# An encoder layer on one core: the queries' squared lengths from products with ones instead of from turned queries

## The chip, the core and the metric

The kernel runs on one core of one Trainium2 chip. The time is the device time of one execution in microseconds; the lower the better. A profile of one execution lists each instruction of the engines: TensorE (PE for its matmuls, PEld for its loads of the stationary operand), VectorE (DVE), ScalarE (ACT), GpSimd (POOL), and SyncE (SP), which here only issues transfers. Each engine works through its own queue in order. SBUF holds 128 partitions; PSUM, where TensorE writes, has 8 banks of 2 KB per partition, that is 512 fp32 numbers.

## What is computed

One layer of an encoder over 1040 tokens (16 learned ones ahead of 1024) with 1024 features: an RMS norm, one wide input projection, two mixers side by side (a gated delta rule over 8 heads of 128 features, run forwards and backwards, and a short convolution), a gated merge, an output projection, and a SwiGLU block. All in fp32. The part that matters here is how the delta rule treats its queries and keys:

```python
def l2norm(t):
    return t * lax.rsqrt(jnp.sum(t * t, axis=-1, keepdims=True) + L2_EPS)

    qkv = jax.nn.silu(depthwise_conv_centred(jnp.concatenate([q, k, v], axis=-1), conv_w)).astype(f32)
    qc, kc, vc = jnp.split(qkv, [DN_QK, 2 * DN_QK], axis=-1)
    qc = l2norm(qc.reshape(Bsz, L, DN_HEADS, DN_DK)) * (DN_DK ** -0.5)
    kc = l2norm(kc.reshape(Bsz, L, DN_HEADS, DN_DK))
...
    o = (o_fwd + o_bwd)[:, META_PAD:]
    o = o * lax.rsqrt(jnp.mean(o * o, axis=-1, keepdims=True) + RMS_EPS) * norm_w.astype(f32)
```

So for each head and token the sum of squares over the 128 features is wanted, of the key and of the query. The query's scale passes linearly to the output `o` of its token, so the kernel leaves queries unscaled and brings their squared length in only when `o` is normed, at the end of the head's scan.

## The kernel before

The first part of the kernel, to about 1062 us, holds the input projection and the whole delta rule. The projection is cut into units of 128 output features (`u_qkv`, `u_short`, `u_gate`, `u_z`). `dense_steps` (L332) runs a unit's matmuls, three fp32r products for each of 8 blocks of 1024 features and each stretch of 320 to 512 tokens; its matmuls are L339. The features come out on the partitions and the tokens along the free dimension, so a head's keys and queries lie as `kT` and `qT`, the two halves of the tile `kq`: 128 features by 1040 tokens.

The work of the heads is put between these matmuls. A head passes through four streams, written as generators: `g_decay` (the decay factors `PQ`, 128x2x128 for each of 8 chunks of 128 tokens; exponentials at L532 on ScalarE), `g_norm` (lengths, and the products of keys with keys and of queries with keys), `g_inv` (the inverse of a triangular block for each chunk, on VectorE with transfers through DRAM, then 32x32 and 64x64 products at L711 to L749) and `g_scan` (the recurrence; matmuls L805 to L840). At each `yield` a stream names the time at which it wants to go on. After each three projection matmuls `run_streams` (L967) resumes every stream whose time has come, and `pump` (L316) hands VectorE jobs of its own (convolutions, the small triangular solves). All of that happens while the program is being written: the times come from the planner's own estimates, kept in `T` by `pe`, `V`, `A` and `on`, and what results is a fixed order of instructions on each engine. The hardware then keeps each engine's order, and semaphores make it wait for what is not ready.

`g_norm` (L537) goes like this. The 16 learned tokens are turned first (L561, L562). Then `tok` (L553) is called for each of four pairs of chunks: it takes a PSUM bank by `psd` (three banks in turn) and turns two chunks of keys and two of queries into it, by TensorE transposes (`transpose`, L97), so that tokens lie on the partitions. ScalarE copies the two turned chunks of keys to `kn` (L580), which the scan needs, and squares all four with a running sum along the free dimension (L550, 128x128, followed by the reading of the accumulator), into the columns `ssk` and `ssq` of `small`. The turned queries are used for nothing else. One `tok` runs ahead of ScalarE's work on the one before.

`kkq` (L587) multiplies a chunk's keys with the chunk's keys and queries together: one fp32 product, 128 stationary columns, 256 moving ones, into a bank by `psd`. Two run ahead (L593). The loop over chunks (L606 to L621) then waits for the chunk's exponentials, has VectorE form the two `NP` blocks from the bank (L612) and multiply `PQ` by its second half (L616), and issues the `kkq` of two chunks on. `ssk` goes into `cc` ahead of the loop (L595 to L599). `ssq` is first read in `norm` at the end of `g_scan` (L883).

Two pools matter beside: `half_buffer` (L351), three buffers of 128x520 in SBUF, taken in turn by the tanh of the convolutions (L366), the short convolutions' sums (L409, L414), the gates (L458) and others; and SyncE's queue, in which the weight loads (L935) stand among the transfers of `g_inv` and the stores.

Of the kernel before, what the change touches and what calls it, by code (L numbers as in the profile page):

```python
# [8 lines left out]
F32 = mybir.dt.float32  # L9
F32R = mybir.dt.float32r  # L10
I32 = mybir.dt.int32
AF = mybir.ActivationFunctionType
# [4 lines left out]
P = 128  # L17
# [3 lines left out]
META = 16  # L21
# [4 lines left out]
NC = 8  # L26
# [21 lines left out]
def encoder_layer(ctx: ExitStack, tc: tile.TileContext, x, meta, norm1_w, w_in, w_ba,  # L48
                  dn_conv_w, A_log, dt_bias, dn_norm_w, sc_conv_w, w_bdn, w_bsc,
                  w_out, norm2_w, w_gu, w_down, final_w, out):  # L50
    nc = tc.nc
# [8 lines left out]
    dr = ctx.enter_context(tc.tile_pool(name="dr", bufs=1, space=DRAM))  # L60
# [3 lines left out]
    def uid(s):  # L64
        cnt["n"] += 1
        return f"{s}_{cnt['n']}"

    def s4(n=1024):
        return tp.tile([P, 1024], F32, tag="s4", name=uid("s4"), bufs=4)[:, :n]
# [4 lines left out]
    def psd():  # L74
        return ps.tile([P, 512], F32, tag="e", name=uid("pe"), bufs=3)
# [18 lines left out]
    mm = nc.tensor.matmul  # L94

    def transpose(dst, src, n=P):
        nc.tensor.transpose(dst, src, ident[:n, :n])  # L97
# [167 lines left out]
    def on(e, ns, ready=0.0):  # L265

        T[e] = max(T[e], ready, T["pe"]) + ns
        return T[e] + TOPE

    def pe(ns):  # L270
        T["pe"] += ns
        return T["pe"] + HOP

    def V(n, kind=0):
        return on("dve", (68 + 1.042 * n, 130 + 1.042 * n, 130 + 0.52 * n)[kind])

    def A(n):
        return on("act", 144 + 0.834 * n)
# [19 lines left out]
    def enqueue(lane, gen):  # L298
        j = Job(gen)
        if not lanes[lane]:  # L300
            spent[lane] = max(spent[lane], min(spent.values()))
        lanes[lane].append(j)
        return j
# [47 lines left out]
    def half_buffer():  # L351
        return d1.tile([P, 520], F32, tag="rb", name=uid("rb"), bufs=3)
# [129 lines left out]
    def cs(c):  # L482
        return slice(META + c * P, META + (c + 1) * P)

    B = lambda b: slice(32 * b, 32 * b + 32)
# [16 lines left out]
    def norm_job(st_, ssk1, cc, ce, he, y, tmp, sk):  # L502
        nc.vector.tensor_tensor(out=ce, in0=cc, in1=he, op=ALU.mult)
        V(18)
        yield T["dve"] + DEP
        rsqrt(y, ssk1, tmp)
        [V(9) for _ in range(11)]
        yield T["dve"] + DEP
        nc.vector.tensor_tensor(out=sk, in0=y, in1=ssk1, op=ALU.mult)
        V(9)  # L510
# [25 lines left out]
    def g_norm(h, st_):  # L536

        kq = st_["kq"]
        kT, qT = kq[:, 0], kq[:, 1]
        small = dn.tile([P, 9, 12], F32, tag="small", name=uid("small"), bufs=2)  # L540
        st_["small"] = small
        ssk, ssq, rk2, ssk1, y, tmp, sk = (small[:, :, i] for i in range(7))
        cc, ce = small[:, :, 7:9], small[:, :, 9:11]
        nc.gpsimd.memset(small, 1.0)
        kn = dn.tile([P, 9, P], F32, tag="kn", name=uid("kn"), bufs=2)
        st_["kn"] = kn

        def square(src, dst, p=P):
            jk = dn.tile([P, P], F32, tag="jk", name=uid("jk"))
            nc.scalar.activation(jk[:p], src, AF.Square, accum_out=dst)  # L550
            return on("act", 400)

        def tok(c2):  # L553
            pt = psd().rearrange("p (c a d) -> p c a d", c=2, a=2)
            for c in range(2):
                for a, s in ((0, kT), (1, qT)):
                    transpose(pt[:, c, a], s[:, cs(2 * c2 + c)])
            return pt, pe(4 * 107)

        pt = psd()  # L560
        transpose(pt[:META, :P], kT[:, 0:META])  # L561
        mm(pt[:META, P:P + META], kT[:, 0:META], kT[:, 0:META], start=True, stop=True)  # L562
        t = pe(120)
        nxt = tok(0)
        yield t
        nc.scalar.copy(kn[:META, 8], pt[:META, :P])
        A(P)
        square(pt[:META, :P], ssk[:META, 8:9], META)
        Nm = dn.tile([META, META], F32, tag="Nm", name=uid("Nm"), bufs=2)
        st_["Nm"] = Nm  # L570
        nc.scalar.copy(Nm, pt[:META, P:P + META])
        A(META)
        nc.gpsimd.tensor_tensor(out=Nm, in0=Nm, in1=Dm[:, h], op=ALU.mult)
        yield T["act"]
        for c2 in range(4):
            pt, t = nxt
            if c2 < 3:
                nxt = tok(c2 + 1)
            yield t
            nc.scalar.copy(kn[:, 2 * c2:2 * c2 + 2], pt[:, :, 0])  # L580
            A(256)
            for c in range(2):
                for a, s in ((0, ssk), (1, ssq)):
                    t = square(pt[:, c, a], s[:, 2 * c2 + c:2 * c2 + c + 1])
            yield T["act"]

        def kkq(c):  # L587
            pk = psd()
            mm(pk[:, :2 * P].rearrange("p (a t) -> p a t", a=2), kT[:, cs(c)], kq[:, :, cs(c)],  # L589
                                  start=True, stop=True)  # L590
            return pk, pe(435)

        nxt = [kkq(0), kkq(1)]  # L593
        yield T["act"] + HOP
        nc.vector.tensor_scalar(out=ssk1, in0=ssk, scalar1=EPS, scalar2=None, op0=ALU.add)  # L595
        nc.vector.reciprocal(rk2, ssk1)
        hb = beta.rearrange("p c (d h) -> p c d h", d=2)[:, :, :, h]
        he = ed.rearrange("p c (d h) -> p c d h", d=2)[:, :, :, h]
        nc.vector.tensor_tensor(out=cc, in0=hb, in1=rk2.unsqueeze(2).broadcast_to([P, 9, 2]), op=ALU.mult)  # L599
        nc.vector.tensor_scalar(out=Nm, in0=Nm, scalar1=cc[:META, 8, 0:1], scalar2=None, op0=ALU.mult)  # L600
        on("dve", 500)
        NP = dn.tile([P, NC, 2, P], F32, tag="NP", name=uid("NP"), bufs=2)
        PQ = st_["PQ"]
        st_["NP"] = NP
        yield T["act"] + HOP - 300
        for c in range(NC):  # L606
            pk, t = nxt.pop(0)
            while c not in st_["exp"]:
                yield T["pe"] + 200
            yield max(t, st_["exp"][c])  # L610
            for d in range(2):
                nc.vector.scalar_tensor_tensor(out=NP[:, c, d], in0=pk[:, 0:P], scalar=cc[:, c, d:d + 1],  # L612
                                               in1=PQ[:, c, d], op0=ALU.mult, op1=ALU.mult)
                V(P, 1)
            yield T["dve"] - 200
            nc.vector.tensor_tensor(out=PQ[:, c], in0=pk[:, P:2 * P].unsqueeze(1).broadcast_to([P, 2, P]), in1=PQ[:, c],  # L616
                                    op=ALU.mult)
            V(2 * P)
            if c + 2 < NC:
                nxt.append(kkq(c + 2))  # L620
            yield T["dve"] - 200  # L621
        enqueue("norm", norm_job(st_, ssk1, cc, ce, he, y, tmp, sk))
# [325 lines left out]
    def start_streams():  # L948
        nonlocal ndec, nnorm, ninv, nscan
        h = ndec  # L950
        if h < H and h < freed + 2 and not decs:
            decs.append([g_decay(h, heads[h]), T["dve"] + HOP, h])
            ndec += 1
        h = nnorm
        if h < H and h < ndec and h < done + 2 and not norms and all(k in heads[h] and heads[h][k]() for k in ("tk", "tq")):
            norms.append([g_norm(h, heads[h]), T["dve"] + HOP, h])
            nnorm += 1
        h = ninv
        if h < H and not invs and heads[h].get("normed"):
            invs.append([g_inv(h, heads[h]), T["dve"] + HOP, h])  # L960
            ninv += 1
        h = nscan
        if h < H and not scans and heads[h].get("inverted") and "tv" in heads[h] and heads[h]["tv"]():
            scans.append([g_scan(h, heads[h]), T["dve"] + HOP, h])
            nscan += 1
# [22 lines left out]
    with tc.tile_pool(name="st", bufs=1) as st:  # L988
# [9 lines left out]
        rows = st.tile([P, 2, P], F32, name="rows")  # L998
# [208 lines left out]
        ones = c1.tile([P, P], F32, name="ones")  # L1207
# [336 lines left out]
    t = KT - 1  # L1544
# [99 lines left out]
    rows = [s4(D) for _ in range(4)] + [rows2[:, t] for t in range(4)]  # L1644
# [129 lines left out]
```

## Time and profile before

| | us |
|---|---|
| Three runs, median | 2010.35 (2009.24 to 2010.55) |
| The profiled execution | 2009.61 |
| its span, first instruction to last | 2007.9 |
| TensorE busy | 1987.4 |
| VectorE busy | 1353.8 |
| ScalarE busy | 823.9 |
| GpSimd busy | 119.6 |

How to read the rows that follow. In the first row the busy time of each engine stands with its share of the span and the number of instructions. A row of a stretch gives the window's start and end, its length, and for PE, PEld, DVE, ACT and POOL the busy time and the number of instructions, then the granted TensorE clock (1.00 is full speed), the share of the DMA engines' time and GB/s. A row of a group names line, engine, operation, out and in, shapes and count, then after a bar the busy time together and the mean of one in ns, then the engine's idle time before them and what ended it. A row of a wait has who waited for whom, the total in us, how often, and the longest. A row of the timeline gives start, duration, engine, line and operation; rows of one kind that follow each other are merged (x4). A matmul's record is longer than the time by which it holds TensorE, as the next one starts while it drains; what it costs is read from the end of one to the end of the next. An fp32 product leaves two matmul records, an fp32 transpose one.

### The profile page before, as it was taken

What the parts mean: (1) busy time and instruction counts of PE and PEld (TensorE: products, weight loads), DVE (VectorE), ACT (ScalarE), POOL (GpSimd) and SP (SyncE); (2) the same over time, 40 slices, a digit from 0 to 9 for tenths busy, and PEclk for the clock granted to TensorE, in tenths of its full rate; (3) what the DMA queues carried; (4) which work ended last, traced back from release to release, by engine and by line L of the source; (5) the groups of instructions that cost most, each with busy time, mean ns of one, the idle gap of its engine ahead of it and who ended that gap; (6) DMA issues with size and microseconds to landing.
All of it is one profiled execution on the core that took longest, in us unless ns stands there. A gap on an engine that the chain in (4) does not pass through costs nothing.

```text
span 2007.9 us, 31943 instructions
## 1 busy us (share of the span) xinstructions
PE 1987.4 (99%) x12059; PEld 1727.9 (86%) x12059; DVE 1353.8 (67%) x2966; ACT 823.9 (41%) x1945; POOL 119.6 (6%) x407
## 2 busy tenths in 40 slices
PE   9999999999999999999999999999999999999998
PEld 8999999999999988988888888887888888888887
DVE  6889586888888776866245434468866666646575
ACT  6462345454554464633334211224423333334344
POOL 2002200101020202010000000000000000000000
PEclk9999999999999999999999999999999999999999
DMA  3121222212212232232127633123666345477654
GB/s 138 40 88 64 75 78 71 74 47 76 59 54 85 69 101 64 81 89 94 70 94 247 215 126 116 58 90 109 237 225 221 139 149 186 158 272 244 196 172 167
DMA packets 131409, 247.85 MB, mean 123 GB/s; under 512 B 45045, under 2 KB 54694, under 8 KB 128823
## 3 DMA queue, kind: packets, MB, share of 16 engines
q1 hardware_dynamic: 130679, 244.77, 36.1%
q8 instruction: 94, 1.54, 0.3%
q10 hardware_dynamic: 576, 1.05, 0.1%
q14 instruction: 60, 0.49, 0.1%
HBM read 179.10 MB, written 66.67 MB: 122 GB/s over the span
## 4 chain that ended last, share of the span: by engine, by line
PE 90%; DVE 5%; ACT 2%; DMA 1%; issue 1%; SPq 0%; ACTq 0%; DVEq 0%
PE pm L339 36%; PE pd L1514 10%; PE pe L1514 4%; PE pm L1514 3%; PE pe L589 1%; PE pd L820 1%; PE pe L134 1%; PE pe L135 1%; PE pe L133 1%; PE pd L840 1%; PE pd L134 1%; PE pd L133 1%; PE pd L135 1%; PE pe L1682 1%; PE pe L1680 1%; PE pd L837 1%
## 5 line engine op out<-in xcount | busy, mean ns | idle before, releaser
L339 PE MATMUL pm<-hTh,wh 128*128 128x512 f32 (+4 forms) x1424 | 518.2, 369 | 0.8 <-ACT kq L391 0.5
L339 PE MATMUL pm<-hTh,wl 128*128 128x512 f32 (+4 forms) x1424 | 483.4, 344 | 0.0
L339 PE MATMUL pm<-al,wh 128*128 128x512 f32 (+4 forms) x1424 | 482.6, 343 | 0.0
L339 PEld LDWEIGHTS pm<-hTh,wh 128*128 128x128 f32 x1424 | 267.0, 188 | 20.4 <-issue 1.7
L339 PEld LDWEIGHTS pm<-hTh,wl 128*128 128x128 f32 x1424 | 266.1, 188 | 19.8 <-DVE wl L942 0.3
L339 PEld LDWEIGHTS pm<-al,wh 128*128 128x128 f32 x1424 | 267.4, 189 | 14.5
L101 DVE TENSOR_TENSOR al<-raw,ring_h 128x1024 fp32r<-128x1024 f32 x73 | 88.8, 1224 | 65.4 <-ACT ring_h L100 64.6
L942 DVE TENSOR_TENSOR wl<-raw,wh 128x512 fp32r<-128x512 f32 x134 | 91.0, 690 | 51.0 <-ACT wh L945 50.5
L100 ACT CAST ring_h<-raw 128x1024 fp32r<-128x1024 f32 x73 | 76.8, 1055 | 106.8 <-PE pd L1682 35.5
L361 DVE SCALAR_TENSOR_TENSOR kq<-ra,wc,kq 128x520 f32<-128x520 f32 x128 | 96.9, 757 | 3.3 <-ACT kq L391 1.7
L945 ACT CAST wh<-raw 128x512 fp32r<-128x512 f32 x134 | 79.2, 622 | 13.3 <-PE pm L339 9.6
L100 ACT CAST wh<-raw 128x1024 fp32r<-128x1024 f32 x43 | 45.2, 1052 | 85.8 <-PE pe L134 35.2
L827 ACT ACTIVATE w<-pd,small 128x128 f32<-128x128 f32 x128 | 40.2, 366 | 84.8 <-PE pd L820 79.7
L498 DVE TENSOR_TENSOR fP<-fP,tm 128x135 f32<-128x135 f32 (+23 forms) x248 | 71.3, 288 | 4.9
L494 DVE TENSOR_TENSOR tm<-fP,fN 128x135 f32<-128x135 f32 (+23 forms) x248 | 71.2, 287 | 4.4
L849 DVE SCALAR_TENSOR_TENSOR S<-S,eGl,pd 128x128 f32<-128x128 f32 x104 | 31.9, 345 | 52.0 <-PE pd L837 33.9
L1516 DVE TENSOR_TENSOR b<-pd,b 128x512 f32<-128x512 f32 x22 | 15.2, 691 | 68.5 <-PE pd L1514 68.5
L1617 ACT ACTIVATE b<-b 128x512 f32<-128x512 f32 x22 | 13.9, 633 | 114.8 <-DVE b L1516 114.8
L101 DVE TENSOR_TENSOR wl<-raw,wh 128x1024 fp32r<-128x1024 f32 x43 | 52.4, 1220 | 12.3 <-ACT wh L100 12.2
L664 POOL TENSOR_TENSOR tm<-mP,mN 1x15 f32<-1x15 f32 (+7 forms) x120 | 42.9, 358 | 218.7 <-DMA mN<-ndm 210.2
L1514 PE MATMUL pd<-b_hl,wh 128*128 128x512 f32 x176 | 54.4, 390 | 0.0
L361 DVE SCALAR_TENSOR_TENSOR vT<-ra,wc,vT 128x520 f32<-128x520 f32 x64 | 48.4, 756 | 3.6 <-ACT vT L391 2.6
(523 smaller groups left out, 4416.9 us busy)
## 6 DMA issues: line engine op xcount, KB each, us to landing
raw<-in_w_in_dram SPq DMA_DIRECT2D x72, 512.0 KB
raw<-in_w_gate_up_dram SPq DMA_DIRECT2D x44, 512.0 KB
sums<-in_w_down_dram SPq DMA_DIRECT2D x22, 512.0 KB
t_d<-sums SPq DMA_DIRECT2D x11, 1024.0 KB
raw<-s_d SPq DMA_DIRECT2D x44, 256.0 KB
raw<-t_d SPq DMA_DIRECT2D x44, 256.0 KB
act_d<-b SPq DMA_DIRECT2D x43, 256.0 KB
raw<-act_d SPq DMA_DIRECT2D x33, 256.0 KB
```

The costliest lines, as they stand in the source:

```text
L100: nc.scalar.copy(hi, src)
L101: nc.vector.tensor_tensor(out=lo, in0=src, in1=hi.bitcast(F32), op=ALU.subtract)
L133: mm(po[:m, :n], wh[:, k, :m], xhk[:, t0:t0 + n], start=(k == 0), stop=False)
L339: mm(po[:, :n], ww[:, k], f(k)[:, t0:t0 + n], start=i == 0, stop=i == 3 * KT - 1)
L361: nc.vector.scalar_tensor_tensor(out=acc, in0=raw[:, h0 + t:h0 + t + hn], scalar=wc[:, t, col:col + 1], in1=acc, op0=ALU.mult, op1=ALU.add)
L494: nc.vector.tensor_tensor(out=tv, in0=fP[:, 0:r, j:j + 1].broadcast_to([P, r, n]), in1=fN[:, j:j + 1, j + 1:32].broadcast_to([P, r, n]), o ...
L498: nc.vector.tensor_tensor(out=fP[:, 0:r, j + 1:32], in0=fP[:, 0:r, j + 1:32], in1=tv, op=ALU.subtract)
L664: nc.gpsimd.tensor_tensor(out=tv, in0=mP[:, 0:j + 1, j:j + 1].broadcast_to([1, j + 1, n]), in1=mN[:, j:j + 1, j + 1:META].broadcast_to([1, ...
L827: nc.scalar.activation(w[d], b1[:, 2 + d], AF.Copy, scale=ce[:, c, d:d + 1])
L942: nc.vector.tensor_tensor(out=u[1][1][:, k], in0=u[2][:, k], in1=u[1][0][:, k].bitcast(F32), op=ALU.subtract)
L945: nc.scalar.copy(u[1][0][:, k], u[2][:, k])
L1514: mm(po, x[:, k], y, start=k + i == 0 and not add_to, stop=k == 3 and i == 2, skip_group_check=add_to)
```

## The change

`tok` turns keys only, four chunks to a bank, in two calls instead of four; ScalarE copies 512 columns at a time to `kn` and squares four chunks of keys. The queries' squared lengths come from a new generator, `norms_of_q`, started ahead of the loop over chunks and resumed once at the head of each step from the second on, for three resumptions:

- step 1: two squares on ScalarE of 512 tokens each of the unturned `qT`, into two buffers of `half_buffer`;
- step 2: a bank by `psd`, and 8 fp32 products. The stationary operand is 128x32 ones, the moving one 128 tokens of squares; product j of each 512 tokens writes to partitions 32j to 32j+31, so that every row of a group of 32 holds the sums over the features for 128 tokens;
- step 3: a copy of the 256 columns to a third buffer, a transfer of one row per group to a DRAM tile `sq_d`, and a transfer back from `sq_d` into the column `ssq` of `small`, 128 partitions of 8 single numbers.

What the generator yields is not looked at: it is resumed where the loop stands.

```diff
-        def tok(c2):
-            pt = psd().rearrange("p (c a d) -> p c a d", c=2, a=2)
-            for c in range(2):
-                for a, s in ((0, kT), (1, qT)):
-                    transpose(pt[:, c, a], s[:, cs(2 * c2 + c)])
+        def tok(c4):
+            pt = psd().rearrange("p (c d) -> p c d", c=4)
+            for c in range(4):
+                transpose(pt[:, c], kT[:, cs(4 * c4 + c)])
             return pt, pe(4 * 107)
+
+        def norms_of_q():
+            sqs = []
+            for i in range(2):
+                sqs.append(half_buffer()[:, :512])
+                nc.scalar.activation(sqs[i], qT[:, META + 512 * i:META + 512 * i + 512], AF.Square)
+                A(512)
+            yield
+            pq = psd()[:, :256].rearrange("p (i t) -> p i t", i=2)
+            for i in range(2):
+                for j in range(4):
+                    mm(pq[B(j), i], ones[:, 0:32], sqs[i][:, j * P:(j + 1) * P], start=True, stop=True)
+            pe(500)
+            yield
+            rows = half_buffer()[:, :256]
+            nc.scalar.copy(rows.rearrange("p (i t) -> p i t", i=2), pq)
+            A(256)
+            sq_d = dr.tile([2, 4, P], F32, name=uid("sq_d"), tag="sq_d", bufs=2)
+            nc.sync.dma_start(sq_d.rearrange("i j t -> j i t"), rows[0:P:32].rearrange("j (i t) -> j i t", i=2))
+            nc.sync.dma_start(ssq[:, 0:NC], sq_d.rearrange("i j t -> t (i j)"))
+            yield
...
-        for c2 in range(4):
+        for c4 in range(2):
             pt, t = nxt
-            if c2 < 3:
-                nxt = tok(c2 + 1)
+            if c4 < 1:
+                nxt = tok(c4 + 1)
             yield t
-            nc.scalar.copy(kn[:, 2 * c2:2 * c2 + 2], pt[:, :, 0])
-            A(256)
-            for c in range(2):
-                for a, s in ((0, ssk), (1, ssq)):
-                    t = square(pt[:, c, a], s[:, 2 * c2 + c:2 * c2 + c + 1])
+            nc.scalar.copy(kn[:, 4 * c4:4 * c4 + 4], pt)
+            A(512)
+            for c in range(4):
+                square(pt[:, c], ssk[:, 4 * c4 + c:4 * c4 + c + 1])
             yield T["act"]
...
+        late = norms_of_q()
         for c in range(NC):
+            if c:
+                next(late, None)
             pk, t = nxt.pop(0)
```

## The prediction

> **What bounds the kernel now.** I read the page's first part, then the busy time by stretch, then what TensorE itself waited for.
>
> ```profile
> PE 1987.4 (99%) x12059; PEld 1727.9 (86%) x12059; DVE 1353.8 (67%) x2966; ACT 823.9 (41%) x1945; POOL 119.6 (6%) x407
> 105.00:873.00 768.00, 764.04 (x6061) 704.56 (x6062) 609.28 (x1718) 373.02 (x1198) 96.86 (x331) 1.00 0.23 71
> 873.00:1062.00 189.00, 189.00 (x1232) 158.42 (x1229) 87.72 (x274) 71.15 (x197) 9.76 (x32) 1.00 0.27 89
> PE pd L820 <- DVE r L815: 3.4, 6, 0.8
> PE pm L339 <- ACT kq L391: 0.5, 2, 0.3
> PE pd L837 <- ACT v L832: 0.2, 1, 0.2
> ```
>
> The stretch 105 to 873 us holds all eight passes through `g_norm`, the only code that changes. TensorE is busy 764.0 of its 768 us at a granted clock of 1.00, ScalarE only 373. So a nanosecond put on TensorE's queue here, or a wait in it, is a nanosecond of the kernel, while time taken off ScalarE pays nothing unless TensorE was waiting for it. The list of TensorE's waits says that it almost never was: 0.5 and 0.2 us. From 873 to 1062 us TensorE runs without a gap on fill units, so no head's tail is exposed at the end of the phase.
>
> **The change part by part.** *Transposes removed.* Per head 8 of the 16 transposes of L97 go (the queries'), 64 in all. One group of four, between projection matmuls (start, duration):
>
> ```profile
> 108.77 0.31 PE L339 MATMUL pm<-hTh,wl 128*128 128x320 f32 x1
> 108.92 0.60 PE L97 MATMUL pe<-ident,kq 128*128 128x128 f32 x4
> 109.27 0.39 PE L339 MATMUL pm<-hTh,wh 128*128 128x320 f32 x1
> 109.50 0.31 PE L339 MATMUL pm<-al,wh 128*128 128x320 f32 x1
> ```
>
> From the end of the one projection matmul (109.08) to the end of the next (109.66) is 0.58 us, of which that next one alone takes 0.15 (109.50 to the start of its successor). Four transposes cost 0.43, one 0.109; 64 cost 7.0 us.
>
> *Products added.* Per head 8 fp32 products: stationary 128x32 ones, 128 moving columns, each to one of four 32-partition column groups, two rounds of four. What an fp32 product costs at full width is in the keys-by-keys product of L589, 256 moving columns, two records:
>
> ```profile
> 128.59 0.34 PE L339 MATMUL pm<-hTh,wl 128*128 128x384 f32 x1
> 128.77 0.59 PE L589 MATMUL pe<-kq 128*128 128x256 f32 x2
> 129.01 0.53 PE L339 MATMUL pm<-hTh,wh 128*128 128x384 f32 x1
> ```
>
> End to end 0.61, less 0.17 for the last: 0.44 for 256 columns, 0.22 for 128. Twice a transpose: eight in a row would be 1.75 us, against 0.87 for the eight transposes removed. So the part pays only if the groups run at once. The nearest rows are the 32x32 products of the block inverse, which use four column groups too, but also four row groups:
>
> ```profile
> 214.74 0.34 PE L339 MATMUL pm<-hTh,wl 128*128 128x384 f32 x1
> 215.01 0.21 PE L711 MATMUL pd<-XT,NP 32*32 32x32 f32 x1
> ...
> 215.57 0.19 PE L711 MATMUL pd<-XT,NP 32*32 32x32 f32 x1
> 215.69 0.45 PE L339 MATMUL pm<-hTh,wh 128*128 128x384 f32 x1
> ...
> L711 PE MATMUL pd<-XT,NP 32*32 32x32 f32 x32 | 0.8, 194 | 0.0
> L711 PE MATMUL pd<-Xe,NP 32*32 32x32 f32 x32 | 0.7, 194 | 0.0
> ```
>
> 64 records start within 0.56 us, 0.009 each, where a quarter of 0.109 would be 0.027 one after another: at least three ran at once. The whole excursion takes 1.06 us (215.08 to 216.14) less 0.17, that is 0.89; the 0.33 beyond the 0.56 is the price of going into the small tiles and out. I take both over: two rounds of 0.22 plus 0.33 are 0.77 a head, 6.2 us, net −0.8. Bounds: without the mode price 3.5 us (net −3.5); with groups that share the rows and so run one after another, 1.75 + 0.33 a head, 16.6 us (net +9.6). I take the first value, since the columns are what keeps outputs apart in L711 as well.
>
> The Trainium skill ("TensorE: Matmul & The Clock Gate", Part 3, measured speedup vs the span model) gives 2.38x for three column tiles of 32, not three or four. By that the eight products would be 1.75/2.38 = 0.74 instead of 0.44, and the sum 2.4 us higher, an estimate; no run so far shows column groups alone.
>
> *ScalarE.* The costs of what goes and comes:
>
> ```profile
> L550 ACT ACTIVATE jk<-pe 128x128 f32<-128x128 f32 x128 | 35.8, 279 | 3.0
> L550 ACT ACTIVATION_READ_ACCUMULATOR jk<-pe 128x1 f32 x128 | 25.3, 197 | 0.0
> L580 ACT COPY kn<-pe 128x256 f32<-128x256 f32 x32 | 11.6, 363 | 0.1
> L904 ACT COPY NP<-pd 128x512 f32<-128x512 f32 x16 | 9.0, 583 | 15.2 <-PE pd L97 15.1
> L1737 ACT ACTIVATE b<-mA 128x512 f32<-128x512 f32 x4 | 2.5, 627 | 0.0
> ```
>
> Gone: 64 squares with their accumulator reads (64 x 0.476 = 30.5) and 32 copies of 0.363 (11.6). Added: 16 copies of 512 (9.3), 16 squares of 512 (10.0), 8 copies of 256 (2.9). ScalarE loses 20 us of 373, none of it on the path. Zero.
>
> *A new wait at the products.* TensorE's queue is in order, and the products stand in it at the start of step 2 of the loop over chunks. They need two 0.63 squares that ScalarE was given at the start of step 1, and a PSUM bank whose last reader is step 1's multiplication of `PQ` on VectorE (L616). Until now the matmul that waits there waits for the reader of a step further back. How late is that reader? The last head, where steps are shortest:
>
> ```profile
> 857.78 0.59 PE L589 MATMUL pe<-kq 128*128 128x256 f32 x2
> 858.91 0.59 PE L589 MATMUL pe<-kq 128*128 128x256 f32 x2
> 860.03 0.59 PE L589 MATMUL pe<-kq 128*128 128x256 f32 x2
> ...
> 857.96 0.42 DVE L616 TENSOR_TENSOR PQ<-pe,PQ 128x256 f32<-128x256 f32 x1
> 858.93 0.42 DVE L616 TENSOR_TENSOR PQ<-pe,PQ 128x256 f32<-128x256 f32 x1
> 859.91 0.42 DVE L616 TENSOR_TENSOR PQ<-pe,PQ 128x256 f32<-128x256 f32 x1
> ...
> 281.40 0.60 DVE L815 SCALAR_TENSOR_TENSOR r<-pd,negEG,vS 128x128 f32<-128x128 f32 x2
> 282.06 0.71 PE L820 MATMUL pd<-r,NP 128*128 128x128 f32 x4 [0.75 <-DVE r L815]
> ```
>
> It ends 0.60, 0.44 and 0.30 us after its step's key product starts (858.38 against 857.78, and so on); the last two rows give 0.06 for the hop. In the changed program's order the new products stand 0.43 to 1.33 us of TensorE work behind that key product, in three of eight heads the minimum 0.43. That is 0 to 0.2 us late. The squares add more where a step is only 1.1 us long and four exponentials precede them (heads 1, 5, 7). I take 0.2 a head, 1.6 us; bounds 0 and 8.
>
> *A new wait one step later.* The next user of the products' bank is the key product of step 2 or 3; it waits for ScalarE's copy of the sums (0.36). Behind it on TensorE stand the projections. In the changed order it follows the products' end by 0.52, 0.68, 3.5, 1.7, 4.8, 0.52, 2.05 and 0.68 us of TensorE work (heads 0 to 7). With ScalarE free the copy needs 0.06 + 0.36 + 0.06 = 0.48, so it just fits; but ScalarE is in order as well, and between squares and copy stand other things:
>
> ```profile
> L390 ACT COPY ra<-pm 128x320 f32<-128x320 f32 x24 | 10.2, 427 | 6.7 <-PE pm L339 6.7
> 163.01 1.29 ACT L532 ACTIVATE PQ<-PQ,negG 128x128 f32<-128x128 f32 x4 [2.60 <-DVE PQ L527]
> ACT PQ L532 <- DVE PQ L527: 14.5, 15, 2.6
> ACT Xe L691 <- DMA NP<-pd: 19.1, 4, 7.7
> 860.83 0.41 ACT L691 COPY Xe<-NP 32x256 f32<-32x256 f32 x1 [5.16 <-DMA NP<-pd]
> ```
>
> Head 0: two evictions (0.43 and 0.54) and two exponentials (1.29 for four), 1.6 us, against 1.3 from the products' start: 0.7 late with copy and hop. Head 1: four exponentials behind a mask addition (14.5/15, about 1 us): 1.2 late. Heads 5 and 7: two exponentials and the same wait: 0.5 each. Head 3: a copy that waits for a product 1.2 us after the sums: 0.5. Heads 4 and 6: the three block copies of L691 to L693, which today wait for a DMA in four heads of eight, 19.1 us in all; in head 6 then a gate's tanh and four exponentials too: 2.5 late without the DMA; head 4 has 4.8 us of cover: 0. Sum 5.9 us; lower bound 0, upper 5.9 plus 5.16 for each of the two, 16.
>
> *SyncE and DMA.* Per head two small transfers, a write to DRAM and a read back of 1024 single values. The second waits in SyncE's queue for the first to land, and a weight load stands behind it:
>
> ```profile
> SPq L679 <- DMA pd<-fP: 34.8, 11, 6.5
> 172.35 7.80 SPq L935 DMA_DIRECT2D raw<-in_w_in_dram  x2
> 182.54 0.62 ACT L945 CAST wh<-raw 128x512 fp32r<-128x512 f32 x1
> ```
>
> Such a wait takes 34.8/11 = 3.2 us, at most 6.5; the load issued at 172.35 is first read at 182.54, 10 us later. Zero; with the cover gone, a late cast delays the next unit by up to 3 us. The sums' consumer is the end of the head's scan, tens of microseconds on. VectorE and GpSimd get no instruction more or less.
>
> *Order.* The planner issues by its own estimates, which change, so the other streams shift. TensorE's old waits in the scans (3.4 + 0.2) may fall or double: 0, bounds ±3.6.
>
> **Sum.** −0.8 + 1.6 + 5.9 = +6.7 on the profiled execution's 2009.61 (its span 2007.9 and 1.7 around it): 2016.3. The median shown, 2010.35, is 0.74 higher: 2017.
>
> **The rivals.** *Groups one after another* (the products decide, from the point where fewer than two run at once): +9.6 in place of −0.8, 2027. For: all four read the same 128 partitions, which no row shows. Against: L711. *The waits are covered*, ScalarE being 20 us lighter and the order planned: −0.8 and at most 2 us of waits, 2010 to 2012, no change. For: 0.5 and 0.2 us of waits for ScalarE today. Against: the planner's books do not hold the products for the squares, nor the next key product for the copy. *Faster*: the waits are covered, the mode price is half, and the shifted scans lose their 3.4 us for VectorE: −2.1 − 3.4, 2005. For: those waits are accidents of placing. Against: nothing in the change aims at them. *ScalarE held by a DMA* in heads 4 and 6: two times 5.16, 2027, on the forecast's side.
>
> **How the numbers follow.** Forecast with its own range 2014.4 to 2024: 0.55. One after another 0.08, the held ScalarE 0.06, no change 0.19, faster 0.12. Four microseconds, 0.2%, is about what a measurement of this kernel can tell from no change. Slower: 0.55 less 0.03 that falls short, plus 0.14: 0.66. Same: 0.22. Faster: 0.12. The range 2008 to 2027 leaves out most of the faster case and the top of the two expensive ones.
>
> **What would show it.** In the profile after: the time between projection matmuls around the ones products, 0.77 if groups overlap, 2.1 if not; in TensorE's waits new rows at the products (for squares or `PQ`) and at the key product (for the copy), together 7 us, most in heads 0, 1 and 6; ScalarE near 804 us busy. The forecast is wrong if these rows sum to under 3 us, or if a weight cast waits for its load.

## The result, and the profile after

| | before | after |
|---|---|---|
| median of the runs | 2010.35 (2009.24 to 2010.68) | 2029.48 (2028.20 to 2032.07) |
| ratio, 95% interval | | 1.0097 (1.0083 to 1.0112) |
| profiled execution's span | 2007.9 | 2026.6 |

The change costs 19.1 us. First the page's part of busy times, then the busy time by stretch for the stretch that holds `g_norm` (from, to, length, then busy time and count of PE, PEld, DVE, ACT and POOL, the granted clock, the DMA share and GB/s), then TensorE's waits in the order of their sum (total, times, longest). All are of the changed kernel, whose lines behind the edit stand 23 further down: the key product is L609, the products with ones L570, the copy of their sums L574, the multiplication of `PQ` L639, the block copies L714 to L716.

```profile
PE 1993.0 (98%) x12123; PEld 1726.7 (85%) x12123; DVE 1353.0 (67%) x2966; ACT 811.1 (40%) x1825; POOL 118.5 (6%) x407
```

```profile
105.00:873.00 768.00, 750.28 (x5869) 688.25 (x5868) 602.49 (x1704) 356.41 (x1069) 95.29 (x329) 0.99 0.23 70
```

```profile
PE pe L609 <- ACT rb L574: 10.7, 3, 6.1
PE pd L843 <- DVE r L838: 4.0, 10, 0.7
...
PE pe L609 <- DVE PQ L639: 1.8, 2, 1.1
...
PE pm L339 <- ACT kq L391: 0.3, 1, 0.3
PE pe L570 <- DVE PQ L639: 0.3, 1, 0.3
```

In the stretch TensorE now stands idle for 17.7 us, where it was 4.0, and its clock is no longer 1.00 throughout. The first row is the largest part of the loss: three waits of the key product for ScalarE's copy of the sums, 10.7 us, two of them long. The first long one, in head 6, in the timeline (start, duration, engine, line, what; in brackets the idle time before it and what ended it): TensorE, then ScalarE.

```profile
749.46 0.39 PE L339 MATMUL pm<-hTh,wl 128*128 128x512 f32 x1
755.91 1.22 PE L609 MATMUL pe<-kq 128*128 128x256 f32 x2 [6.06 <-ACT rb L574]
756.57 0.99 PE L339 MATMUL pm<-hTh,wh 128*128 128x512 f32 x1
757.36 0.63 PE L339 MATMUL pm<-al,wh 128*128 128x512 f32 x1
...
758.99 0.39 PE L339 MATMUL pm<-hTh,wl 128*128 128x512 f32 x1
759.22 0.39 PE L339 MATMUL pm<-hTh,wh 128*128 128x512 f32 x1
```

```profile
744.97 0.61 ACT L968 CAST wh<-raw 128x512 fp32r<-128x512 f32 x1
751.45 0.41 ACT L714 COPY Xe<-NP 32x256 f32<-32x256 f32 x1 [5.87 <-DMA NP<-pd]
...
752.79 0.60 ACT L458 ACTIVATE rb<-pm 128x512 f32<-128x512 f32 x1
754.33 1.28 ACT L532 ACTIVATE PQ<-PQ,negG 128x128 f32<-128x128 f32 x4 [0.94 <-DVE PQ L527]
755.51 0.35 ACT L574 COPY rb<-pe 128x256 f32<-128x256 f32 x1
```

The copy itself waits for nothing. It is late because ScalarE is in order: block copies of the head before stand in front of it and wait 5.87 us for their transfer, and a gate's tanh and four exponentials come between. The second long wait, in head 7, has the same victim and another cause:

```profile
859.53 0.69 ACT L532 ACTIVATE PQ<-PQ,negG 128x128 f32<-128x128 f32 x2 [1.12 <-DVE PQ L527]
864.51 0.37 ACT L574 COPY rb<-pe 128x256 f32<-128x256 f32 x1 [4.28 <-DMA tb_d<-rb]
```

```profile
864.93 1.22 PE L609 MATMUL pe<-kq 128*128 128x256 f32 x2 [4.35 <-ACT rb L574]
```

Here it is the copy's destination. `rows` is one of the three `rb` buffers that turn, and the one whose turn it is still holds a gate's output that is being stored to `tb_d`.

Both waits cost more than their idle time. The busy time in stretches of 5 us, columns as above, shows the granted clock in the eleventh place:

```profile
750.00:755.00 5.00, 0.00 (x0) 0.00 (x0) 3.79 (x9) 2.48 (x7) 0.00 (x0) 0.71 0.46 103
755.00:760.00 5.00, 4.09 (x12) 3.32 (x13) 3.29 (x10) 0.86 (x4) 0.00 (x0) 0.61 0.42 106
760.00:765.00 5.00, 5.00 (x175) 3.88 (x174) 0.61 (x2) 0.52 (x2) 0.47 (x4) 1.00 0.00 0
...
865.00:870.00 5.00, 5.00 (x16) 4.04 (x17) 2.57 (x8) 1.39 (x4) 0.00 (x0) 0.69 0.45 54
870.00:875.00 5.00, 5.00 (x24) 4.12 (x23) 4.78 (x13) 2.03 (x5) 0.00 (x0) 1.00 0.14 52
```

After each idle stretch the clock is 0.61 and 0.69, and the key product takes 1.22 instead of 0.59. From its start at 755.91 to the projection at 758.99, 3.08 us pass for one key product and five projections; at full speed they take 0.44 + 5 x 0.23 = 1.6. That is 1.5 us more, and in head 7 about as much again. The waits of 1.1 us are followed by no drop. The kernel before has a drop as well, in a later part of the program, behind three waits close together, of 2.63, 0.63 and 0.32 us between 1390.2 and 1395.2:

```profile
1395.00:1400.00 5.00, 4.83 (x16) 3.92 (x17) 3.85 (x7) 1.25 (x2) 0.00 (x0) 0.72 0.70 262
```

So the clock can fall without one long wait. The Trainium skill ("TensorE: Matmul & The Clock Gate", Part 1) says that an idle window of about 3.4 us sets the clock back to half. The drops after 6.06 and 4.35 us and the clock of 1.00 after 1.1 us agree with that; the drop behind three waits, the longest of 2.63 us, says that it is not the least length of one wait.

So the two waits account for 10.4 us idle and some 3 us of slow clock. That leaves near 6 us which no single row of this profile shows.

### The profile page after: what moved, and what is told of

It reads as the page before. It is cut to its first block, busy times and chain, and to the rows that moved or that the text cites. A ratio compares the mean times of both kernels' runs of the same rounds, so it can differ in the third digit from the quotient of the medians.

```text
span 2026.6 us, 31985 instructions
## 1 busy us (share of the span) xinstructions
PE 1993.0 (98%) x12123; PEld 1726.7 (85%) x12123; DVE 1353.0 (67%) x2966; ACT 811.1 (40%) x1825; POOL 118.5 (6%) x407
## 4 chain that ended last, share of the span: by engine, by line
PE 81%; DVE 10%; DMA 3%; ACT 3%; issue 1%; POOL 0%; SPq 0%; ACTq 0%; DVEq 0%; POOLq 0%
PE pm L339 30%; PE pd L1537 10%; PE pe L1537 4%; PE pm L1537 3%; PE pe L134 1%; PE pe L133 1%; PE pe L135 1%; PE pd L843 1%; PE pe L609 1%; PE pd L134 1%; PE pd L133 1%; PE pd L135 1%; PE pe L1705 1%; PE pe L1704 1%; PE pe L1703 1%
## 5 line engine op out<-in xcount | busy, mean ns | idle before, releaser
L339 PE MATMUL pm<-hTh,wh 128*128 128x384 f32 (+4 forms) x1424 | 520.0, 370 | 0.6 <-ACT kq L391 0.3
L339 PE MATMUL pm<-hTh,wl 128*128 128x384 f32 (+4 forms) x1424 | 483.5, 344 | 0.0
L339 PE MATMUL pm<-al,wh 128*128 128x384 f32 (+4 forms) x1424 | 483.1, 344 | 0.0
L101 DVE TENSOR_TENSOR wl<-raw,wh 128x1024 fp32r<-128x1024 f32 x43 | 52.4, 1218 | 13.8 <-ACT wh L100 13.7
L609 PE MATMUL pe<-kq 128*128 128x256 f32 x128 | 39.4, 401 | 12.6 <-ACT rb L574 10.7
```

The lines of the kernel that those rows point to most:

```text
L101: nc.vector.tensor_tensor(out=lo, in0=src, in1=hi.bitcast(F32), op=ALU.subtract)
L339: mm(po[:, :n], ww[:, k], f(k)[:, t0:t0 + n], start=i == 0, stop=i == 3 * KT - 1)
```

## The experiments

Each ratio is against runs of the kernel before on the same chip; the median of these was between 2009.5 and 2010.0. A difference in us between two runs is that of their medians.

**Whose wait is it? (free_bank, own_rows, no_transfers, no_lengths)** Four edits of the changed kernel. *free_bank* cuts the tie between the products' bank and the copy:

```diff
-            nc.scalar.copy(rows.rearrange("p (i t) -> p i t", i=2), pq)
+            nc.scalar.copy(rows.rearrange("p (i t) -> p i t", i=2), sqs[0][:, :256].rearrange("p (i t) -> p i t", i=2))
```

> ScalarE's copy behind the ones products reads the squares in SBUF instead of the sums in PSUM; every instruction, transfer, buffer and the order on each engine stay, the sums of the queries' squares are not read (the queries' lengths are left out of the result). Only the tie between the products' bank and that copy is gone. Theory (TensorE's key product waits for the bank until the copy, and the copy waits in ScalarE's order): the rows of the key product behind L574 vanish; of the 14.7 us that the key products take longer than before and the 1.0 us of slow clock behind them, about 2 us come back in head 6, where the next key product then waits for VectorE, itself held by the transfer NP<-pd: 2013 to 2017 us. Rival (the products and the change of tile size on TensorE cost the time) and rival (the two small transfers cost it) and rival (the replanned order costs it): all of that is still there, 2027 to 2030 us.

Measured: 2015.66, ratio 1.0032 (1.0019 to 1.0045). TensorE's waits, from its list:

```profile
PE pd L843 <- DVE r L838: 3.8, 10, 0.7
...
PE pe L609 <- DVE PQ L639: 2.0, 2, 1.1
...
PE pm L339 <- DVE wl L965: 1.1, 1, 1.1
```

No row of L609 behind L574 is left, and 13.8 us are gone, with every instruction still there. What comes back is as expected in size, but half of it in a place that was not named: a projection waits for the low part of its weight tile, because VectorE too was held by `NP<-pd`.

*own_rows* gives the copy a destination of its own:

```diff
-            rows = half_buffer()[:, :256]
+            rows = dn.tile([P, 256], F32, tag="rq", name=uid("rq"), bufs=1)
```

> The copy of the sums writes a buffer of its own instead of one of the three that turn (rb); nothing else changes, and nothing is left out. Theory: in head 7 the copy waited 4.28 us for a gate's store out of rb, and TensorE 4.35 us behind it; that goes, with about 0.6 us for the key product at half speed and 1.2 us of slow clock after it: 6 us less, 2023 to 2024 us, and in head 6 the wait of 6.06 us stays. Rival (the copy is late in both heads because ScalarE as a whole is held, whatever the buffer): 2028 to 2030 us, and the wait in head 7 stays above 3 us.

Measured: 2024.14, ratio 1.0070 (1.0055 to 1.0085), 5.3 us less and just above its range. TensorE's waits, then two stretches, the first in head 6 and the second in head 7:

```profile
PE pe L609 <- ACT rq L574: 6.1, 2, 5.8
```

```profile
755.00:760.00 5.00, 4.52 (x11) 3.60 (x12) 2.88 (x9) 0.43 (x2) 0.00 (x0) 0.54 0.39 102
...
865.00:870.00 5.00, 5.00 (x24) 4.01 (x23) 2.99 (x8) 2.97 (x7) 0.00 (x0) 1.00 0.47 65
```

Head 6 keeps its wait and its slow clock, head 7 loses both: the slow clock follows the idle time, not the place in the program.

*no_transfers* leaves out the two transfers of the sums:

```diff
-            nc.sync.dma_start(sq_d.rearrange("i j t -> j i t"), rows[0:P:32].rearrange("j (i t) -> j i t", i=2))
-            nc.sync.dma_start(ssq[:, 0:NC], sq_d.rearrange("i j t -> t (i j)"))
```

> The two transfers of the sums (to DRAM and back into ssq) are left out, so the queries' lengths do not reach the result; the copy, the products and the order on TensorE, VectorE and ScalarE stay. Theory: the transfers of head 6 are issued after the wait that costs 6.06 us, so they cannot be its cause: 2027 to 2030 us, both long waits of the key product still there. Rival (the small transfers delay NP<-pd or a weight load): both waits shrink below 2 us and the time falls below 2020 us.

Measured: 2029.57, ratio 1.0099 (1.0084 to 1.0114). The transfers cost nothing.

*no_lengths* leaves out squares, products, copy and transfers, and keeps the buffers, the banks and the planner's books.

> All of the queries' lengths are left out: no squares, products, copy or transfers, while buffers, banks and the planner's books stay, so the remaining instructions come in the changed kernel's order. It prices the removal alone. Theory: the 64 transposes that went are worth 6 to 7 us, the scans' waits in the new order cost up to 2 us: 2003 to 2006 us. Rival (the replanned order costs the time): 2010 us or more.

Measured: 2011.32, ratio 1.0008 (0.9999 to 1.0017). A miss, and it shows where the other 6 us are: without any of the new work, and with 64 transposes fewer, the kernel is no faster than before. What is left of the change is the order of everything else, with the keys' transposes four to a bank: that must cost what the transposes save.

**The order by itself (old_order_keys).** In the kernel before, the queries' transposes and squares are left out while their entries in the planner's books stay, so that all else is issued as before.

```diff
-                for a, s in ((0, kT), (1, qT)):
+                for a, s in ((0, kT),):
                     transpose(pt[:, c, a], s[:, cs(2 * c2 + c)])
...
-                for a, s in ((0, ssk), (1, ssq)):
-                    t = square(pt[:, c, a], s[:, 2 * c2 + c:2 * c2 + c + 1])
+                t = square(pt[:, c, 0], ssk[:, 2 * c2 + c:2 * c2 + c + 1])
+                on("act", 400)
```

> The kernel before with the queries' transposes and their squares left out (the queries' lengths are left out of the result) and nothing else: the planner's books are kept, so that every other instruction stands in the order of before. The same removal in the order of after (no_lengths) gave 2011.32. Theory formed on that run (the removal is worth its transposes, and the new order gives that back through late weight casts in heads 6 and 7, 2.7 us, waits in the scans, 1.7, and at the key products, 2.0): here 7 us less than before, 2002 to 2004 us. Rival (the transposes were covered, their removal is worth nothing in any order): 2008 to 2011 us.

Measured: 2004.83, ratio 0.9974 (0.9965 to 0.9983). The time is just above its range. The removal is worth 5.2 us against the kernel before, most of the 7.0 expected, and the order of after costs 2011.32 − 2004.83 = 6.5 us. This order includes the keys' transposes four to a bank; no run separates the two. The profiled executions allow a look at the first part of the program alone, from the start of the first projection matmul to the end of the last: 16.77 to 1061.11 in the kernel before, 18.21 to 1055.04 in old_order_keys, 17.61 to 1062.48 in no_lengths. That is 7.5 us for the removal and 8.0 for the order; what lies outside differs by about 2 us from one of them to another.

In TensorE's lists of waits, no_lengths has these rows:

```profile
PE pd L843 <- DVE r L838: 3.9, 10, 0.7
...
PE pe L609 <- DVE PQ L639: 2.3, 3, 1.1
...
PE pm L339 <- DVE wl L965: 1.4, 1, 1.4
PE pm L339 <- ACT wh L968: 0.8, 1, 0.8
```

and old_order_keys has only the first of them, at its own line:

```profile
PE pd L820 <- DVE r L815: 3.5, 6, 1.0
...
PE pm L339 <- ACT kq L391: 0.3, 1, 0.3
```

These rows differ by 4.9 us: 2.3 at the key product, 2.2 at projections that wait for weights, 0.4 in the scans. All of TensorE's idle time in the stretch differs by 5.4 us, 9.03 in no_lengths against 3.61 in old_order_keys:

```profile
105.00:873.00 768.00, 758.97 (x6026) 697.35 (x6025) 610.30 (x1731) 350.34 (x1055) 93.44 (x331) 1.00 0.24 71
```

```profile
105.00:873.00 768.00, 764.39 (x6065) 703.68 (x6064) 613.93 (x1734) 351.81 (x1074) 96.49 (x331) 1.00 0.24 72
```

What goes beyond that is not TensorE waiting there, and no run shows where it comes from. In head 6, where the wait for the low weights (wl) and one of those at the key product lie, VectorE is late: in the new order it is given the block work long before its transfer has landed. Its waits for `NP<-pd`, in no_lengths and in the kernel before:

```profile
DVE XT L718 <- DMA NP<-pd: 12.3, 5, 5.6
```

```profile
DVE XT L695 <- DMA NP<-pd: 6.4, 4, 2.8
```

**Do the four column groups run at once? (one_group)** As free_bank, but all eight products write partitions 0 to 31. Their bank is cut into four slots of 128 sums for that.

```diff
-                    mm(pq[B(j), i], ones[:, 0:32], sqs[i][:, j * P:(j + 1) * P], start=True, stop=True)
+                    mm(pq[B(0), j], ones[:, 0:32], sqs[i][:, j * P:(j + 1) * P], start=True, stop=True)
```

> As free_bank (2015.66), but all eight ones products write one column group, partitions 0 to 31, so that they cannot run at once; the sums are not read (the queries' lengths are left out of the result). Theory (four column groups run at once, as the starts of the 16 records in the profile say): the products take 8 x 0.22 + 0.33 = 2.1 us a head in place of 0.77, 1.3 us a head more, 2025 to 2027 us. Rival (the groups took turns anyway, and the products were cheap for another reason): 2014 to 2018 us.

Measured: 2023.84, ratio 1.0071 (1.0057 to 1.0084), 8.2 us above free_bank and below its range, which lay 9 to 11 above. In head 0 the changed kernel, then one_group, between projections:

```profile
124.46 0.34 PE L339 MATMUL pm<-hTh,wl 128*128 128x384 f32 x1
124.73 0.64 PE L570 MATMUL pe<-rb,ones 128*32 128x128 f32 x16
125.31 0.44 PE L339 MATMUL pm<-hTh,wh 128*128 128x384 f32 x1
```

```profile
124.84 0.34 PE L339 MATMUL pm<-hTh,wl 128*128 128x384 f32 x1
125.11 1.93 PE L570 MATMUL pe<-rb,ones 128*32 128x128 f32 x16
126.97 0.44 PE L339 MATMUL pm<-hTh,wh 128*128 128x384 f32 x1
```

From end to end less 0.17 for the projection: 0.78 against 2.06 us, the predicted 0.77 and 2.08. If the four groups run fully at once, the changed kernel takes the time of two products here and one_group that of eight. The difference of 1.28 us is then six products, 0.21 each, close to the 0.22 read from the key product. The 1.3 us a head, 10.2 in all, are there; that the time rose by only 8.2 fits in part the row of the weight wait, which had cost free_bank 1.1 us and is missing here.

**The copy ahead of the block copies (copy_first, copy_first_own).** In the changed kernel ScalarE's copy is issued right behind the products instead of one step later; the order of the other engines stays. copy_first_own has the buffer of own_rows as well.

```diff
             pe(500)
-            yield
             rows = half_buffer()[:, :256]
             nc.scalar.copy(rows.rearrange("p (i t) -> p i t", i=2), pq)
+            yield
             A(256)
```

> The changed kernel with one instruction moved: ScalarE's copy of the sums is issued right behind the products instead of one step later. The order on TensorE, VectorE and SyncE is the same; on ScalarE only the eight copies move ahead, in head 6 ahead of the three block copies that wait for NP<-pd. Nothing is left out. Theory: the wait of 6.06 us in head 6 goes, with 0.6 us of the slow key product and 1.1 us of slow clock, and about 1 to 3 us come back there as late weight casts and as a wait for VectorE, both held by the same transfer (free_bank showed them); in head 7 the copy still waits for the buffer rb, 4 us: 2023 to 2027 us. Rival (head 6 waits for the transfer itself, wherever the copy stands): 2028 to 2031 us with a wait of 5 us or more in head 6.

> copy_first and own_rows together: the copy of the sums right behind the products, into a buffer of its own. Nothing is left out. Theory: both long waits gone without taking the tie away, so the time comes to that of free_bank (2015.66): 2015 to 2019 us, no wait of the key product for ScalarE above 1 us. Rival (the tie itself costs, also with a timely copy): 2020 us or more.

Measured: copy_first 2022.69, ratio 1.0061 (1.0044 to 1.0078), just below its range; copy_first_own 2016.51, ratio 1.0030 (1.0019 to 1.0041). ScalarE of copy_first_own in head 6:

```profile
746.03 0.37 ACT L573 COPY rq<-pe 128x256 f32<-128x256 f32 x1 [2.08 <-PE pe L570]
749.62 0.41 ACT L715 COPY Xe<-NP 32x256 f32<-32x256 f32 x1 [3.22 <-DMA NP<-pd]
```

The block copies still wait for their transfer, but the copy is out by then, and TensorE has no wait for it anywhere. Two small edits take off 13.0 of the 19.1 us without leaving anything out.

**The products behind the last key product (last_steps, old_order_late).** The three parts of `norms_of_q` move into the last three steps of the loop: in last_steps with the planner of after, in old_order_late with the books of before, as in old_order_keys.

```diff
-            if c:
+            if c > 4:
                 next(late, None)
```

> The changed kernel with the three parts of the queries' lengths placed in the last three steps of the loop over chunks: the products come behind the head's last key product, so that no key product of that head waits for their bank. Nothing is left out. Theory: no row of the key product behind L574 over 1 us; what is left is what free_bank showed (late weight casts and VectorE held by NP<-pd), and the order shifts once more: 2008 to 2016 us. Rival (the waits come from ScalarE being behind, wherever the products stand): 2022 to 2030 us, with TensorE's longest wait for ScalarE's copy over 3 us at whatever uses the bank next.

> The changed kernel's way of finding the queries' lengths in the order of before: the planner's books as before, the queries' transposes and squares out, squares, products, copy and transfers put into the last three steps of the loop over chunks, so that no key product of the head stands behind the bank. Nothing is left out. Theory: old_order_keys (2004.83) plus 0.77 us a head, 6.2 us, and up to 3 us of waits for the squares (last_steps showed 1.6 and 0.7): 2011 to 2014 us. That would say that the method is worth nothing against the transposes even in the best place. Rival (the method itself is cheaper and only the new order cost time): 2004 to 2008 us.

Measured: last_steps 2016.75, ratio 1.0030 (1.0018 to 1.0042), a little above its range; old_order_late 2010.17, ratio 1.0000 (0.9991 to 1.0009), between its two. In both no key product waits for the copy. With the products in the same place, the order of after costs 6.6 us more than that of before. In the order of before, the change's way of finding the lengths costs as much as the transposes that it replaces.

**The block copies given out later (late_blocks).** One number of the planner in `g_inv`:

```diff
-        yield T["pe"] + 5600
+        yield T["pe"] + 11600
         yield from take("inv")
```

> The changed kernel with the planner's allowance between the issue of NP<-pd and the block copies raised from 5600 to 11600 of its ns; nothing else is edited, though the planner then places other work anew as well. Nothing is left out. Theory (in head 6 ScalarE and VectorE were given the block copies 6 us before their transfer had landed): their waits for NP<-pd fall below 3 us in all, the long wait of the key product in head 6 goes, and unless the new places hold one of their own the time falls by 6 us or more: 2013 to 2024 us. Rival (the transfer is late because of something that moves with it, so a later place only moves the wait): 2027 to 2032 us, with a wait of 5 us or more for NP<-pd on ScalarE.

Measured: 2012.06, ratio 1.0011 (1.0001 to 1.0021), better than its range. ScalarE's list has no wait for `NP<-pd` left, VectorE's this one and one of 0.2:

```profile
DVE XT L718 <- DMA NP<-pd: 1.0, 1, 1.0
```

That the whole order shifts with this number is part of the result: the scans' waits fell as well, from 4.0 to 1.7 us, so not all of the 17.4 us can be put down to the block copies.

**Another way to the sums (columns_bf16).** In the order of before, the squares are rounded to bf16 and made the stationary operand, 128 squares by 128 tokens; the moving operand is one column of ones. Each product then leaves 128 sums on 128 partitions, where `ssq` wants them.

```diff
...
+            if c == 5:
+                pq = nxt[-1][0][:, 256:264]
+                for i in range(NC):
+                    mm(pq[:, i:i + 1], qs[:, i * P:(i + 1) * P], ones_b[:, 0:1], start=True, stop=True)
+            if c == 6:
+                nc.scalar.copy(ssq[:, 0:NC], pq)
...
```

> A candidate in the order of before: the squares of the queries are written in bf16, each chunk's 128 squares by 128 tokens are the stationary operand of one product with a single column of ones, so that the eight sums of a head land with the tokens on the partitions, in spare columns of the last key product's bank; one small copy puts them into ssq, with no transfer, no tile of another size and no extra bank. Nothing is left out; only the rounding of the squares differs. Theory: as old_order_keys plus eight short products a head. Their price lies between 0.03 us (a 32x32 product's share) and 0.11 us (a transpose) each, 2 to 7 us in all: 2005 to 2010 us, without new waits of TensorE above 1 us in phase 1. Rival (each pays the price of a change of kind, 0.3 us a head or more, and the bank's copy comes late): 2010 to 2016 us.

Measured: 2005.27, ratio 0.9976 (0.9968 to 0.9985), faster than both kernels. TensorE in head 0:

```profile
131.59 0.59 PE L592 MATMUL pe<-kq 128*128 128x256 f32 x2
132.02 0.34 PE L627 MATMUL pe<-ones_b,qs 128*128 128x1 bf16 x8
132.22 0.39 PE L339 MATMUL pm<-hTh,wh 128*128 128x322 f32 x1
132.46 0.31 PE L339 MATMUL pm<-al,wh 128*128 128x322 f32 x1
```

From the end of the key product (132.18) to that of the projection (132.61), less its own 0.15, is 0.28 us for eight products, against 0.78 for the products with ones: no small tiles to enter, no transfer, no bank of their own.

## Why the prediction was wrong, step by step

The prediction named the right engine, the right stretch and the right wait, and forecast 6.7 us where 19.1 came.

- *What bounds the kernel*: right. The loss is TensorE's idle time in the stretch named, and what ScalarE has less to do (811.1 us busy, not the 804 forecast, from 823.9) bought nothing.
- *TensorE's work, −0.8*: right. The products cost 0.78 us a head against 0.77; old_order_late, which has this term with hardly another, is level with the kernel before. The transposes were worth 5.2 us by the medians and 7.5 in the first part of the profiles, against 7.0. The Trainium skill ("TensorE: Matmul & The Clock Gate", Part 3, "Measured speedup vs the span model") has 2.38x for three column tiles, which would have made it 2.4 us worse, an estimate. Here the eight products took 0.78 us in four groups and 2.06 in one, 2.6 times as long; with the 0.33 for the small tiles taken off both, which is an estimate, it is 0.45 against 1.73, 3.8 times.
- *The wait at the products, +1.6*: 0.3 us, one row; over-sized.
- *The wait for the copy, +5.9*: **the step that failed.** The mechanism is shown (free_bank takes it away), the size was not. Heads 0, 1 and 5, given 2.4 us together, have no such wait; head 3, given 0.5, has one of 0.3. In head 6 the prediction saw the block copies in front of the copy and took 2.5 us "without the DMA", though the DMA's wait on that very line was quoted (19.1 us in four heads); with it there were 6.06. The 2027 us that went with it stood as a rival at 0.06. In head 7 it took 0.5 for exponentials; the 4.35 us came from a buffer that the copy writes, which the working did not look at: it asked what the copy reads and who stands ahead of it, not where it puts its result. The upper bound of 16 covered the sum of 10.7, the chosen value did not.
- *Not in the sum at all*: the slow clock after each long wait, about 1.5 us twice. A wait on TensorE was priced at its own length.
- *Order, 0 ± 3.6*: **the second step that failed.** It cost 6.3 to 6.6 us by the medians (copy_first_own and last_steps against old_order_late; no_lengths against old_order_keys), the keys' transposes four to a bank included. The bound was made from the only waits that the old order had, those of the scans; the new order made waits of other kinds, at key products and at weights, where the old one had none.
- *SyncE and DMA, zero*: right (no_transfers). The weight cast that waits, named as a sign of error, did not come; but in four experiments (free_bank, no_lengths, copy_first, copy_first_own) a projection waited 0.6 to 1.4 us for a cast. The engine of the cast was behind there because it had waited for `NP<-pd`, not for a load.
- *Rivals*: groups one after another is refuted (one_group). The held ScalarE was right for head 6 and wrong for head 4.

Laid out as a chain of runs from the changed kernel back to the one before: 13.0 for the two waits and their clock (to copy_first_own), 6.3 for the order (to old_order_late, which also has the products in a later place), −0.2 for the method (against 2010.35). They add up to 19.1 because each is the difference of two neighbours in the chain; that is no check of their causes. What stays open is the share of the order that is not a wait of TensorE in the stretch, what the keys' transposes four to a bank have to do with it, and how much of late_blocks' gain was aimed at and how much fell to it.

## What to carry to other kernels

A new instruction on an idle engine is not free if the bottleneck waits for it: ask for each such instruction what it reads, what it writes, and what stands ahead of it in the queue, and take the waits already in that queue at their full measured length. Free the shared resource (a bank, a buffer) before work that waits for a transfer is given out, or behind the last user who could stand in line for it. When a planner places the work, an edit that alters its books is two changes: keep the books for one run, so that the price of the order and the price of the work come apart.

## What the hardware showed that was not expected

- A TensorE idle for 4.35 or 6.06 us comes back at half the granted clock for some microseconds (0.50 from 756 to 758 and from 865 to 868 us; the key product 1.22 us in place of 0.59), and each such pause cost about 1.5 us beside its length. Three waits of 2.63, 0.63 and 0.32 us within 5 us brought a drop too, a single one of 1.1 us did not.
- Eight fp32 products over all 128 rows took 0.78 us in four 32-column groups and 2.06 in one. With 0.22 us a product from the key product's row, entering and leaving the small tiles took about 0.3 us whether the groups overlapped (0.78 − 0.44) or not (2.06 − 1.75), an estimate.
- Eight bf16 products with a 128x128 stationary operand and one moving column held up the projections by 0.28 us, 0.035 each, less than the 0.109 of an fp32 transpose of the same 128x128.
